# Residual rows and the mixer's first weight tiles loaded behind chosen steps of the down projection

## The chip, the core and the metric

The kernel runs on one core of one Trainium2 chip. The metric is the device time of one execution in microseconds (us); of several executions the median counts. TensorE (PE) does the matrix products, ScalarE (ACT), VectorE (DVE) and GpSimd (POOL) the elementwise work, and SyncE (SP) issues nearly all the transfers between the chip's memory (HBM) and the on-chip SBUF, in one fixed order.

## The reference

One encoder layer in float32 on 1024 rows of 1024 numbers, in three residual blocks and a last norm:

```
x = x + 0.5 * swiglu(rms_norm(x), ffn1_w_in, ffn1_w_out)
x = x + mixer(rms_norm(x), w_in_mix, w_out_mix)
x = x + 0.5 * swiglu(rms_norm(x), ffn2_w_in, ffn2_w_out)
x = rms_norm(x)
```

`swiglu` is `(silu(gate) * up) @ w_out`, with gate and up the halves of `h @ w_in` and an inner width of 2816. The mixer projects the normed rows with `w_in_mix` and runs attention and a gated recurrence on the result. The change touches the two down projections (`@ w_out`) and the loads of the mixer's first weight tiles.

## The kernel before, in words

**Numbers.** Each float32 operand is split into a rounded high part and the rest (`split`, L101): ACT casts the high part (L104), DVE subtracts it from the source for the low part (L105). A product is then three matmuls: high by high, high by low, low by high.

**The down projection** (`ffn_down`, L443) multiplies the 1024 x 2816 activations by the 2816 x 1024 weights. Rows and columns are each halved, and the four quarter results come from seven products in place of eight (the Strassen-Winograd scheme). They run in this order, with their operands' names: A11·B11, A12·B21, S2·T2, A22·T4, S3·T3, S1·T1, S4·B22. Each has 11 steps (`NPAIR`), and a step has 4 row tiles of 3 matmuls, so a product is 132 matmuls. `product` (L524) calls `operands` (L466) for each step, which loads the raw tile of the left operand (`raw_out`, pool `draw`, 4 buffers), loads or builds the right one, and splits both into one of 5 buffers (`ab`; 6 in the second feed-forward block). The left operands A come from `d_act`, the sums S from `d_comb`, both in HBM. Right-hand tiles that serve several products stay in SBUF (`kept` tiles). T2, T4 and T3 are built by POOL from kept tiles (L485 to L495). The profile's names drop the numbers, so A11, A12 and A22 all read `raw_out_ffn_A`, and S1 to S4 read `raw_out_ffn_S`; the PSUM banks tell them apart: `pya` belongs to A11, then S2, then S3, `pyb` to A12, `pyc` to A22, `pyd` to S1, `pye` to S4.

**The residual rows.** The result is added to eight row tiles `x[0]` to `x[7]` of 128 x 1024, on DVE (`add`, L538): the even tiles take A11 and A12, then S2 and S1, the odd ones A22, S3 and S1, and S4 closes the even ones. `rows_in` (L548) loads four of them at a time (512 KB each). It is a hook: a function called after the step whose number it has. The two calls are

```
        product(("A11", "B11"), a, True, {2: [rows_in(0)]})
        product(("A12", "B21"), b, True, {0: [add(0, lo, a)]})
        product(("S2", "T2"), a, False, {0: [add(0, lo, b)], 4: [rows_in(1)]})
```

**The mixer's first weights.** `load_split` (L154) loads a raw tile of 512 KB (L157) into one of three buffers and splits it. `done1` (L1264) asks for two tiles of the recurrence's weights (`raw_rec_w`) once row tile 0 is done; the third and the first tiles of the next projection (`raw_ri_w`) are asked for in the mixer (L639, L688), which PE reaches after the down projection.

**What sets the order.** The program is scheduled when it is built: a planner takes the instructions in the order of the code, with its own idea of time, and writes down a fixed order for each engine. A load with nothing to wait for is moved ahead as far as its buffer and the planner allow, whatever place in the code asked for it. On an engine the order is then fixed: an instruction that waits holds everything behind it, on SP too. `tc.issue_after(ins)` ties what is inside it: it may not be placed ahead of `ins` on that engine. In `operands`, it already keeps the loads of kept tiles behind the step's first load.

## Time and profile before

| what | value |
|---|---|
| median of 3 runs | 2008.72 us (2003.79 to 2009.0) |
| the profiled execution | 2008.14 us |
| its span, first to last instruction | 2006.0 us |
| PE busy | 1944.5 us, 97% of the span |
| DVE, ACT, POOL busy | 1329.7, 807.4, 727.2 us |
| mean granted TensorE clock | 0.991 |
| moved by DMA | 259.34 MB, 129 GB/s on average |

The profiled execution is 2.14 us longer than its span, and 0.58 us shorter than the median. In the timelines, a row is a run of equal instructions: its start, its length, the engine, the line, what is written from what, how often, and in brackets how long the engine had been idle before it and what ended that. SPq stands for SP's queue: a row there is the issue of a transfer, not the transfer. In the rows of windows, a time with (x...) behind it is an engine's busy time and its instruction count; the granted clock, the share of the 16 DMA engines that was busy (just over 1 where the records overlap) and GB/s come last. Line numbers are those of the kernel before.

### The profile page before, as it was taken

What the parts mean: (1) busy time and instruction counts of PE and PEld (TensorE: products, weight loads), DVE (VectorE), ACT (ScalarE), POOL (GpSimd) and SP (SyncE); (2) the same over time, 40 slices, a digit from 0 to 9 for tenths busy, and PEclk for the clock granted to TensorE, in tenths of its full rate; (3) what the DMA queues carried; (4) which work ended last, traced back from release to release, by engine and by line L of the source; (5) the groups of instructions that cost most, each with busy time, mean ns of one, the idle gap of its engine ahead of it and who ended that gap; (6) DMA issues with size and microseconds to landing.
All of it is one profiled execution on the core that took longest, in us unless ns stands there. A gap on an engine that the chain in (4) does not pass through costs nothing.

```text
span 2006.0 us, 26914 instructions
## 1 busy us (share of the span) xinstructions
PE 1944.5 (97%) x10157; PEld 1665.6 (83%) x10157; DVE 1329.7 (66%) x1941; ACT 807.4 (40%) x1269; POOL 727.2 (36%) x543
## 2 busy tenths in 40 slices
...
GB/s 206 142 117 78 116 120 96 79 100 278 303 147 131 152 32 39 47 74 33 105 64 156 138 161 113 64 210 167 138 100 105 105 100 95 77 186 331 184 121 158
DMA packets 219594, 259.34 MB, mean 129 GB/s; under 512 B 12596, under 2 KB 150088, under 8 KB 219464
## 3 DMA queue, kind: packets, MB, share of 16 engines
...
HBM read 185.21 MB, written 72.35 MB: 128 GB/s over the span
## 4 chain that ended last, share of the span: by engine, by line
PE 85%; DMA 6%; DVE 4%; ACT 2%; issue 1%; POOL 1%; SPq 0%; DVEq 0%; ACTq 0%; POOLq 0%
PE pa_ffn L311 16%; PE pd_ffn L311 11%; PE rec_ps L168 6%; PE pya_ffn L515 6%; PE pc_ffn L311 6%; PE pb_ffn L311 5%; PE pye_ffn L515 3%; PE pyd_ffn L515 3%; PE pyc_ffn L515 3%; PE lv L738 2%; PE pa L1032 2%; PE pp_ffn L295 2%; PE ri_ps L649 2%; PE aq_ps L649 2%; PE rg_ps L649 2%; PE py L1032 2%
## 5 line engine op out<-in xcount | busy, mean ns | idle before, releaser
L105 DVE TENSOR_TENSOR hl_in_ffn_A<-raw_in_ffn,hl_in_ffn_A 128x512 fp32r<-128x512 f32 x135 | 200.4, 1489 | 98.6 <-ACT hl_in_ffn_A L104 98.6
L311 PE MATMUL pa_ffn<-ffn_T,hl_in_ffn_S 128*128 128x512 f32 x984 | 242.7, 389 | 0.0
L311 PE MATMUL pd_ffn<-ffn_B,hl_in_ffn_S 128*128 128x512 f32 x960 | 232.7, 389 | 0.0
L311 PEld LDWEIGHTS pa_ffn<-ffn_T,hl_in_ffn_S 128*128 128x128 f32 x984 | 184.7, 188 | 38.4
L311 PEld LDWEIGHTS pd_ffn<-ffn_B,hl_in_ffn_S 128*128 128x128 f32 x960 | 180.2, 188 | 37.4
L105 DVE TENSOR_TENSOR hl_in_ffn_S<-s_ffn,hl_in_ffn_S 128x512 fp32r<-128x512 f32 x164 | 148.0, 907 | 64.1 <-ACT hl_in_ffn_S L104 63.7
L104 ACT CAST hl_in_ffn_S<-s_ffn 128x512 fp32r<-128x512 f32 x164 | 101.6, 622 | 220.2 <-PE pd_ffn L311 167.9
L104 ACT CAST hl_in_ffn_A<-raw_in_ffn 128x512 fp32r<-128x512 f32 x135 | 83.5, 625 | 155.0 <-PE pc_ffn L311 75.0
L105 DVE TENSOR_TENSOR hl_out_ffn_S<-raw_out_ffn_S,hl_out_ffn_S 128x512 fp32r<-128x512 f32 (+1 forms) x88 | 102.8, 1173 | 50.5 <-ACT hl_out_ffn_S L104 50.4
L105 DVE TENSOR_TENSOR hl_out_ffn_A<-raw_out_ffn_A,hl_out_ffn_A 128x1024 fp32r<-128x1024 f32 (+1 forms) x66 | 92.8, 1416 | 55.5 <-ACT hl_out_ffn_A L104 55.0
L273 POOL TENSOR_TENSOR s_ffn<-s_ffn,raw_in_ffn 128x512 f32<-128x512 f32 x41 | 65.7, 1602 | 172.1 <-issue 115.9
L515 PE MATMUL pya_ffn<-hl_out_ffn_S 128*128 128x512 f32 x528 | 122.8, 393 | 4.2 <-DVE hl_out_ffn_S L105 4.2
L168 PE MATMUL rec_ps<-hm,hl_rec_w 128*128 128x512 f32 x528 | 121.6, 390 | 1.9 <-DVE hm L152 1.9
L515 PEld LDWEIGHTS pya_ffn<-hl_out_ffn_S 128*128 128x128 f32 x528 | 100.0, 190 | 26.3 <-DVE hl_out_ffn_S L105 5.5
L311 PE MATMUL pb_ffn<-ffn_B,hl_in_ffn_A 128*128 128x512 f32 x492 | 119.8, 389 | 0.0
L311 PE MATMUL pc_ffn<-ffn_T,hl_in_ffn_A 128*128 128x512 f32 x492 | 118.8, 389 | 0.3 <-DVE hl_in_ffn_A L105 0.3
L311 PE MATMUL pa_ffn<-ffn_B,hl_in_ffn_A 128*128 128x512 f32 x492 | 119.0, 389 | 0.0
L104 ACT CAST hl_out_ffn_S<-raw_out_ffn_S 128x512 fp32r<-128x512 f32 (+1 forms) x88 | 73.5, 837 | 108.4 <-PE pya_ffn L515 41.1
L168 PEld LDWEIGHTS rec_ps<-hm,hl_rec_w 128*128 128x128 f32 x528 | 98.5, 188 | 22.3 <-DVE hm L152 2.2
L311 PEld LDWEIGHTS pc_ffn<-ffn_T,hl_in_ffn_A 128*128 128x128 f32 x492 | 92.3, 188 | 19.8 <-DVE hl_in_ffn_A L105 0.7
L311 PEld LDWEIGHTS pb_ffn<-ffn_B,hl_in_ffn_A 128*128 128x128 f32 x492 | 92.3, 188 | 19.2
L311 PEld LDWEIGHTS pa_ffn<-ffn_B,hl_in_ffn_A 128*128 128x128 f32 x492 | 92.3, 188 | 19.2
...
## 6 DMA issues: line engine op xcount, KB each, us to landing
raw_in_ffn<-in_ffn_w_in SPq DMA_DIRECT2D x88, 512.0 KB, 4.2
raw_out_ffn_S<-d_comb SPq DMA_DIRECT2D x88, 256.0 KB, 2.7
d_comb<-g_ffn POOLq DMA_DIRECT2D x82, 256.0 KB, 2.3
raw_out_ffn_A<-d_act SPq DMA_DIRECT2D x66, 256.0 KB, 5.4
ffn_kept<-in_ffn_w_out SPq DMA_DIRECT2D x65, 256.0 KB, 5.6
d_act<-g_ffn SPq DMA_DIRECT2D x62, 256.0 KB, 2.3
raw_out_ffn_A<-in_ffn_w_out SPq DMA_DIRECT2D x52, 256.0 KB, 4.1
x<-d_x SPq DMA_DIRECT2D x24, 512.0 KB, 5.5
```

The lines of the kernel that those rows point to most:

```text
L104: nc.scalar.copy(hl[:, 0, :], src)
L105: (lo_engine or nc.vector).tensor_sub(hl[:, 1, :], src, hl[:, 0, :].bitcast(F32))
L168: nc.tensor.matmul(out, hl[:, a, ks], h[half][b][:, k, cols], start=(k == 0 and i == 0), stop=(k == NK - 1 and i == 2),)
L273: nc.gpsimd.tensor_sub(s2, s1, a11)
L295: nc.tensor.matmul(halves(ps[j]), A[2 * j + k // 4][:, a, ks], B[k // 4][:, :, b, k % 4, lo:hi], start=(k == 0 and i == 0), stop=(k == NK ...
L311: nc.tensor.matmul(ps, A[:, a, ks], op(key)[:, b, k, :], start=(first and k == 0 and i == 0), stop=(k == 3 and i == 2), skip_group_check=True,
L515: nc.tensor.matmul(ps, hl[:, a, j * P : (j + 1) * P], hl[:, b, hi], start=(first and i == 0 and n == 0), stop=(i == last and n == 2), skip ...
L649: nc.tensor.matmul(ps[:, tt, :], h[half][a][:, k, ts], hl[k // 4][:, b, ws], start=(k == 0 and i == 0), stop=(k == NK - 1 and i == 2),)
L738: nc.tensor.matmul(pl[:, cs], now[:, 0, cs], now[:, 1, cs], start=True, stop=True)
L1032: nc.tensor.matmul(py, lhs(a, n), units[n][:, b, ds], start=(n == 0 and i == 0), stop=(n == 3 and i == 2),)
```

## The change

Three loads get a tie on SP's queue.

- `row_in` loads one row tile behind the raw load of the step at which it is called (`step_load`). `rows_in` now spreads the four calls over the steps 3, 5, 7 and 9 of A11·B11 for the even tiles, and over the same steps of A22·T4 for the odd ones.
- The mixer's first two weight tiles are asked for by a hook, `ahead`, at step 1 of S3·T3, and no longer in `done1`.
- `gate`, set there to that step's raw load, holds every load of `load_split` behind it until the mixer's input part is built. That holds the third recurrence tile and the `raw_ri_w` tiles back too.
- The first add of S3·T3 is called after step 2, not step 0.

The instructions are the same ones in number and size; only orders differ. The diff, without the line that sets `gate` to None at the start:

```
@@ -103,6 +104,10 @@
         nc = self.nc
         nc.scalar.copy(hl[:, 0, :], src)
         (lo_engine or nc.vector).tensor_sub(hl[:, 1, :], src, hl[:, 0, :].bitcast(F32))
+
+    def behind(self, load):
+
+        return self.tc.issue_after(load.ins) if load else nullcontext()
 
     def gain_row(self, name):
         g = self.gpool.tile([P, D], F32, name=f"g_{name}", tag="gain")
@@ -154,7 +159,8 @@
     def load_split(self, src, shape, name, pool=None, tag="whl", lo_engine=None):
 
         raw = self.wpool.tile([P, 1024], F32, name=f"raw_{name}", tag="raw")
-        self.nc.sync.dma_start(raw.rearrange("p (a b) -> p a b", b=shape[1]), src)
+        with self.behind(self.gate):
+            self.nc.sync.dma_start(raw.rearrange("p (a b) -> p a b", b=shape[1]), src)
         hl = (pool or self.wpool).tile([P, 2, 1024], F32R, name=f"hl_{name}", tag=tag)
         self.split(hl, raw, lo_engine)
         return hl
@@ -440,7 +446,7 @@
                 mid()
         next(before)
 
-    def ffn_down(self, name, act, comb, slots, load, done, follow, finish, tail):
+    def ffn_down(self, name, act, comb, slots, load, done, follow, finish, tail, ahead):
 
         nc = self.nc
         w_out = self.io[f"{name}_w_out"]
@@ -467,7 +473,7 @@
             nm = f"{name}_{keys[0]}_{i}"
             left, right = keys
             raw = self.draw.tile([P, 2, 512], F32, name=f"raw_out_{nm}", tag="raw")
-            first = fetch(raw[:, 0], left, i)
+            first = self.step_load = fetch(raw[:, 0], left, i)
             kept = None
             if right == "B11":
                 if i < 4:
@@ -545,19 +551,24 @@
                     )
             return run
 
-        def rows_in(odd):
+        def row_in(t):
             def run():
-                for j in range(4):
-                    x[2 * j + odd] = load(2 * j + odd)
+                with self.behind(self.step_load):
+                    x[t] = load(t)
             return run
 
+        def rows_in(odd, first, hooks):
+            for j in range(4):
+                hooks.setdefault(first + 2 * j, []).append(row_in(2 * j + odd))
+            return hooks
+
         a, b = banks("pya"), banks("pyb")
-        product(("A11", "B11"), a, True, {2: [rows_in(0)]})
+        product(("A11", "B11"), a, True, rows_in(0, 3, {}))
         product(("A12", "B21"), b, True, {0: [add(0, lo, a)]})
-        product(("S2", "T2"), a, False, {0: [add(0, lo, b)], 4: [rows_in(1)]})
+        product(("S2", "T2"), a, False, {0: [add(0, lo, b)]})
         c = banks("pyc")
-        product(("A22", "T4"), c, True, {0: [add(0, hi, a)]})
-        product(("S3", "T3"), a, False, {0: [add(1, lo, c, -1.0)]})
+        product(("A22", "T4"), c, True, rows_in(1, 3, {0: [add(0, hi, a)]}))
+        product(("S3", "T3"), a, False, {1: [ahead], 2: [add(1, lo, c, -1.0)]})
         d = banks("pyd")
         product(("S1", "T1"), d, True, {0: [add(1, lo, a), add(1, hi, a)]})
         e = banks("pye")
@@ -1179,7 +1190,8 @@
         out, x_in = rows(io["out"]), rows(io["x"])
         keys = ("B11", "B21", "T2", "B22", "T4", "T3", "T1")
 
-        def ffn(ctx, name, xn_pair, load, done, d_spec, opened, early_lo, follow, finish, mid=None, tail=2, early=2):
+        def ffn(ctx, name, xn_pair, load, done, d_spec, opened, early_lo, follow, finish, mid=None, tail=2, early=2,
+                ahead=lambda: None):
             def sbuf(c, key, bufs, **kw):
                 return c.enter_context(
                     tc.tile_pool(name=f"{name}_{key}", bufs=bufs, reuse_waits="tile", **kw)
@@ -1213,7 +1225,7 @@
                 slots = [t[:, j, :] for t in tiles for j in range(shape[1])] + extra
                 k.ffn_down(
                     name, act, comb, slots, lambda t: load(pools, t), lambda t, x: done(pools, t, x),
-                    follow, finish, tail,
+                    follow, finish, tail, ahead,
                 )
 
         hstack = ExitStack()
@@ -1265,8 +1277,10 @@
                 nc.sync.dma_start(d["x1"][t], x)
                 xns[t] = pools["xn"].tile([P, D], F32, name=f"xn_n1_{t}", tag="xn")
                 k.norm_rows(x, gain_m[0], xns[t], f"n1_{t}", HALVES)
-                if t == 0:
-                    k.rec_hls = [k.rec_weights(0, j) for j in range(2)]
+
+            def ahead1():
+                k.gate = k.step_load
+                k.rec_hls = [k.rec_weights(0, j) for j in range(2)]
 
             def follow1(t):
                 if not hm:
@@ -1279,12 +1293,13 @@
                     follow1(t)
 
             ffn(c1, "ffn1", pair1, load1, done1, dict(x=8, xn=3), opened1, nc.vector, follow1, finish1,
-                lambda: k.vectors(k.raw), tail=3, early=1)
+                lambda: k.vectors(k.raw), tail=3, early=1, ahead=ahead1)
 
         with ExitStack() as c2:
             pools = open_pools(c2, tc, "m1", st=2, t4=2, v=1, x=1, A=1, rope=1, tot=1, q=2, f=1)
             k.open_psum(c2, "m1", pp=(2, 1024), ph=(2, 1024))
             k.mixer_in(hm, pools, d)
+            k.gate = None
 
         with hstack, ExitStack() as c3:
             pools = open_pools(
```

**Place 1: SP, from the end of the first up projection into A11.** Names carry their numbers here: `raw_out_ffn1_A11_4` is the raw tile of step 4 of A11, `raw_rec_w_0_0` to `_2` are the three recurrence tiles, `ffn1_kept` a kept tile, `d_act21` the last activations going out. Before:

```order
L157 DMA raw_rec_w_0_0_5448<-in_w_in_mix 128x8x128
L157 DMA raw_rec_w_0_1_5453<-in_w_in_mix 128x8x128
L157 DMA raw_rec_w_0_2_5747<-in_w_in_mix 128x8x128
L464 DMA raw_out_ffn1_A11_4_3863<-d_act8_103 128x512
L464 DMA ffn1_kept0_3771<-in_ffn1_w_out 128x512
L464 DMA raw_out_ffn1_A11_5_3883<-d_act10_105 128x512
L464 DMA ffn1_kept0_3771<-in_ffn1_w_out 128x512
L464 DMA raw_out_ffn1_A11_6_3903<-d_act12_107 128x512
L464 DMA ffn1_kept0_3771<-in_ffn1_w_out 128x512
L376 DMA d_act21_116<-g0_ffn1_21_3649 128x512
L464 DMA raw_out_ffn1_A11_7_3923<-d_act14_109 128x512
```

In the changed kernel:

```order
L470 DMA raw_out_ffn1_A11_4_3857<-d_act8_103 128x512
L470 DMA ffn1_kept0_3771<-in_ffn1_w_out 128x512
L470 DMA raw_out_ffn1_A11_5_3877<-d_act10_105 128x512
L470 DMA ffn1_kept0_3771<-in_ffn1_w_out 128x512
L470 DMA raw_out_ffn1_A11_6_3899<-d_act12_107 128x512
L470 DMA ffn1_kept0_3771<-in_ffn1_w_out 128x512
L382 DMA d_act21_116<-g0_ffn1_21_3649 128x512
L470 DMA raw_out_ffn1_A11_7_3919<-d_act14_109 128x512
```

The three recurrence tiles no longer stand ahead of A11's step 4. The three `raw_ri` tiles, which stood behind step 7, are gone from here as well. All six now stand in the S3 product: the recurrence tiles between the raw loads of steps 1 and 2, the `raw_ri` tiles between those of steps 3 and 5. On ACT and on DVE the splits of the recurrence tiles moved from between steps 3 and 4 of A11 to the seam of A22 and S3: tiles 0 and 1 ahead of S3's step 0, tile 2 ahead of its step 1.

**Place 2: SP, in the second half of A12.** `x0_0` to `x0_7` are the residual row tiles. Before:

```order
L464 DMA ffn1_kept2_3773<-in_ffn1_w_out 128x512
L1247 DMA x0_0_3837<-in_x 128x1024
L1247 DMA x0_2_3839<-in_x 128x1024
L1247 DMA x0_4_3841<-in_x 128x1024
L1247 DMA x0_6_3843<-in_x 128x1024
L464 DMA raw_out_ffn1_A12_7_4151<-d_act15_110 128x512
L464 DMA raw_out_ffn1_A12_7_4151<-in_ffn1_w_out 128x512
L464 DMA ffn1_kept2_3773<-in_ffn1_w_out 128x512
L1247 DMA x0_1_4340<-in_x 128x1024
L464 DMA raw_out_ffn1_A12_8_4171<-d_act17_112 128x512
L464 DMA raw_out_ffn1_A12_8_4171<-in_ffn1_w_out 128x512
L464 DMA ffn1_kept2_3773<-in_ffn1_w_out 128x512
```

In the changed kernel:

```order
L470 DMA ffn1_kept2_3773<-in_ffn1_w_out 128x512
L1259 DMA x0_0_3855<-in_x 128x1024
L1259 DMA x0_2_3897<-in_x 128x1024
L1259 DMA x0_4_3939<-in_x 128x1024
L1259 DMA x0_6_3981<-in_x 128x1024
L470 DMA raw_out_ffn1_A12_7_4151<-d_act15_110 128x512
L470 DMA raw_out_ffn1_A12_7_4151<-in_ffn1_w_out 128x512
L470 DMA ffn1_kept2_3773<-in_ffn1_w_out 128x512
L470 DMA raw_out_ffn1_A12_8_4171<-d_act17_112 128x512
L470 DMA raw_out_ffn1_A12_8_4171<-in_ffn1_w_out 128x512
L470 DMA ffn1_kept2_3773<-in_ffn1_w_out 128x512
```

The even tiles stand where they stood, between steps 6 and 7. Of the odd ones, `x0_1` stood here, and the other three stood between these rows and the end of A12; all four stand in A22 now, after the raw loads of steps 3, 5, 7 and 9. In the second block it is the same: the even rows stay at step 6 of A12, the odd ones move from steps 6 and 7 of A12 to A22.

**Place 3: DVE, at the start of S2.** A split of a step of S2 has two subtractions, one from its raw tile and one from its kept tile; `x0_0<-pyb` and the like are the adds of the finished A12 product. Before:

```order
L105 TENSOR_TENSOR hl_out_ffn1_S2_0_4235<-raw_out_ffn1_S2_0_4231,hl_out_ffn1_S2_0_4235 128x512
L542 SCALAR_TENSOR_TENSOR x0_0_3837<-pyb_ffn1_0_3779,x0_0_3837 128x512
L542 SCALAR_TENSOR_TENSOR x0_2_3839<-pyb_ffn1_1_3780,x0_2_3839 128x512
L105 TENSOR_TENSOR hl_out_ffn1_S2_1_4260<-raw_out_ffn1_S2_1_4256,hl_out_ffn1_S2_1_4260 128x512
L542 SCALAR_TENSOR_TENSOR x0_4_3841<-pyb_ffn1_2_3781,x0_4_3841 128x512
L105 TENSOR_TENSOR hl_out_ffn1_S2_0_4235<-ffn1_kept2_3773,hl_out_ffn1_S2_0_4235 128x512
L542 SCALAR_TENSOR_TENSOR x0_6_3843<-pyb_ffn1_3_3782,x0_6_3843 128x512
L105 TENSOR_TENSOR hl_out_ffn1_S2_2_4281<-raw_out_ffn1_S2_2_4277,hl_out_ffn1_S2_2_4281 128x512
L105 TENSOR_TENSOR hl_out_ffn1_S2_1_4260<-ffn1_kept2_3773,hl_out_ffn1_S2_1_4260 128x512
L105 TENSOR_TENSOR hl_out_ffn1_S2_3_4302<-raw_out_ffn1_S2_3_4298,hl_out_ffn1_S2_3_4302 128x512
L105 TENSOR_TENSOR hl_out_ffn1_S2_2_4281<-ffn1_kept3_3774,hl_out_ffn1_S2_2_4281 128x512
```

In the changed kernel:

```order
L106 TENSOR_TENSOR hl_out_ffn1_S2_0_4235<-raw_out_ffn1_S2_0_4231,hl_out_ffn1_S2_0_4235 128x512
L106 TENSOR_TENSOR hl_out_ffn1_S2_1_4260<-raw_out_ffn1_S2_1_4256,hl_out_ffn1_S2_1_4260 128x512
L106 TENSOR_TENSOR hl_out_ffn1_S2_0_4235<-ffn1_kept2_3773,hl_out_ffn1_S2_0_4235 128x512
L106 TENSOR_TENSOR hl_out_ffn1_S2_2_4281<-raw_out_ffn1_S2_2_4277,hl_out_ffn1_S2_2_4281 128x512
L106 TENSOR_TENSOR hl_out_ffn1_S2_1_4260<-ffn1_kept2_3773,hl_out_ffn1_S2_1_4260 128x512
L106 TENSOR_TENSOR hl_out_ffn1_S2_3_4302<-raw_out_ffn1_S2_3_4298,hl_out_ffn1_S2_3_4302 128x512
L548 SCALAR_TENSOR_TENSOR x0_0_3855<-pyb_ffn1_0_3779,x0_0_3855 128x512
L106 TENSOR_TENSOR hl_out_ffn1_S2_2_4281<-ffn1_kept3_3774,hl_out_ffn1_S2_2_4281 128x512
L548 SCALAR_TENSOR_TENSOR x0_2_3897<-pyb_ffn1_1_3780,x0_2_3897 128x512
L548 SCALAR_TENSOR_TENSOR x0_4_3939<-pyb_ffn1_2_3781,x0_4_3939 128x512
L548 SCALAR_TENSOR_TENSOR x0_6_3981<-pyb_ffn1_3_3782,x0_6_3981 128x512
L106 TENSOR_TENSOR hl_out_ffn1_S2_3_4302<-ffn1_kept3_3774,hl_out_ffn1_S2_3_4302 128x512
```

The four adds moved back: both halves of steps 0 and 1 are split ahead of them now, where three of them stood ahead of step 0's second half. In the second block they moved in the same way.

More of the change, by code (lines that the diff above doesn't have):

```diff
@@ L105, in split, with behind @@
         (lo_engine or nc.vector).tensor_sub(hl[:, 1, :], src, hl[:, 0, :].bitcast(F32))
+    def behind(self, load):
+        return self.tc.issue_after(load.ins) if load else nullcontext()
     def gain_row(self, name):
@@ L156, in load_split @@
         raw = self.wpool.tile([P, 1024], F32, name=f"raw_{name}", tag="raw")
-        self.nc.sync.dma_start(raw.rearrange("p (a b) -> p a b", b=shape[1]), src)
+        with self.behind(self.gate):
+            self.nc.sync.dma_start(raw.rearrange("p (a b) -> p a b", b=shape[1]), src)
         hl = (pool or self.wpool).tile([P, 2, 1024], F32R, name=f"hl_{name}", tag=tag)
```

39 lines of the change are left out of this document (23 added, 16 removed).

## Prediction

> **What bounds the kernel now.** I read the page first, then the timeline of PE through both down projections, then the windows and the queues at the places where PE falls behind.
>
> ```profile
> span 2006.0 us, 26914 instructions
> ...
> PE 1944.5 (97%) x10157; PEld 1665.6 (83%) x10157; DVE 1329.7 (66%) x1941; ACT 807.4 (40%) x1269; POOL 727.2 (36%) x543
> ```
>
> PE is the bound. A change of order can win only what PE loses, and the change touches the two down projections alone. PE's timeline there, the first block, then the second:
>
> ```profile
> 463.21 11.04 PE L515 MATMUL pya_ffn<-hl_out_ffn_A 128*128 128x512 f32 x48
> ...
> 494.26 19.20 PE L515 MATMUL pyb_ffn<-hl_out_ffn_A 128*128 128x512 f32 x84
> ...
> 529.10 1.09 PE L515 MATMUL pya_ffn<-hl_out_ffn_S 128*128 128x512 f32 x4
> 532.30 30.89 PE L515 MATMUL pya_ffn<-hl_out_ffn_S 128*128 128x512 f32 x128 [2.11 <-DVE hl_out_ffn_S L105]
> 563.02 30.08 PE L515 MATMUL pyc_ffn<-hl_out_ffn_A 128*128 128x512 f32 x132
> 592.94 30.08 PE L515 MATMUL pya_ffn<-hl_out_ffn_S 128*128 128x512 f32 x132
> ```
>
> ```profile
> 1783.78 30.08 PE L515 MATMUL pya_ffn<-hl_out_ffn_A 128*128 128x512 f32 x132
> 1813.70 22.85 PE L515 MATMUL pyb_ffn<-hl_out_ffn_A 128*128 128x512 f32 x100
> ...
> 1844.66 1.07 PE L515 MATMUL pya_ffn<-hl_out_ffn_S 128*128 128x512 f32 x4
> 1846.84 3.01 PE L515 MATMUL pya_ffn<-hl_out_ffn_S 128*128 128x512 f32 x12 [1.11 <-DVE hl_out_ffn_S L105]
> 1850.82 26.61 PE L515 MATMUL pya_ffn<-hl_out_ffn_S 128*128 128x512 f32 x116 [0.96 <-DVE hl_out_ffn_S L105]
> 1877.26 30.08 PE L515 MATMUL pyc_ffn<-hl_out_ffn_A 128*128 128x512 f32 x132
> ```
>
> Each product is 132 matmuls, so the distance from one product's start to the next is its cost. Undisturbed it is 592.94 - 563.02 = 29.92 us, or 2.72 a step. In the first block A11 takes 31.05, A12 34.84 and S2 33.92: 1.13 + 4.92 + 4.00 = 10.05 us lost. In the second the same three take 29.92, 30.96 and 32.60: 0 + 1.04 + 2.68 = 3.72. The ceiling of the gain is thus 13.77 us. Why PE waits shows in the windows (the last three columns are granted clock, DMA share, GB/s):
>
> ```profile
> 463.00:500.00 37.00, 36.44 (x160) 29.55 (x159) 23.21 (x29) 18.42 (x25) 13.93 (x9) 1.00 1.01 355
> 500.00:531.00 31.00, 27.09 (x112) 20.10 (x110) 21.49 (x17) 10.78 (x13) 16.70 (x11) 1.00 0.98 362
> ...
> 596.00:630.00 34.00, 34.00 (x152) 28.15 (x151) 20.33 (x27) 16.18 (x26) 3.84 (x3) 1.00 0.33 93
> ...
> 1815.00:1850.00 35.00, 33.02 (x143) 26.26 (x142) 23.40 (x20) 12.92 (x17) 18.45 (x13) 1.00 0.94 335
> ```
>
> Through A11 and A12 the DMA engines are full, in S3 two thirds idle. Among what fills them are loads that nobody needs there. SP's queue, and the sizes:
>
> ```profile
> 463.40 2.22 SPq L157 DMA_DIRECT2D raw_rec_w<-in_w_in_mix  x3
> ...
> 473.76 1.70 SPq L157 DMA_DIRECT2D raw_ri_w<-in_w_in_mix  x3
> ...
> 501.59 2.80 SPq L1247 DMA_DIRECT2D x<-in_x  x4
> ...
> 506.29 0.45 SPq L1247 DMA_DIRECT2D x<-in_x  x1
> ...
> 511.40 0.99 SPq L1247 DMA_DIRECT2D x<-in_x  x2
> ...
> 515.38 0.33 SPq L1247 DMA_DIRECT2D x<-in_x  x1
> ```
>
> ```profile
> ffn_kept<-in_ffn_w_out SPq DMA_DIRECT2D x65, 256.0 KB, 5.6
> ...
> x<-in_x SPq DMA_DIRECT2D x16, 512.0 KB, 7.0
> ...
> raw_rec_w<-in_w_in_mix SPq DMA_DIRECT2D x12, 512.0 KB, 3.9
> ```
>
> **The change part by part.** *Mixer tiles out of A11.* ACT shows what they hold up, and SP's own waits what holds them:
>
> ```profile
> 472.44 1.05 ACT L104 CAST hl_rec_w<-raw_rec_w 128x1024 fp32r<-128x1024 f32 x1 [2.15 <-DMA raw_rec_w<-in_w_in_mix]
> 473.40 0.62 ACT L104 CAST hl_out_ffn_A<-raw_out_ffn_A 128x512 fp32r<-128x512 f32 x1
> ...
> 512.82 1.05 ACT L104 CAST hl_out_ffn_A<-raw_out_ffn_A 128x1024 fp32r<-128x1024 f32 x1 [6.10 <-DMA raw_out_ffn_A<-in_ffn_w_out]
> ```
>
> ```profile
> SPq L157 <- DVE hl_ri_w L105: 70.4, 4, 35.6
> ...
> SPq L157 <- PE pa_ffn L311: 15.8, 1, 15.8
> ```
>
> SP stood 15.8 us at the first tile's load, until the up projection's last matmul let its buffer go; step 4 of A11 was queued behind. ACT then cast the three tiles before step 4, which it reached at 473.40, while PE, four steps past 463.21, wanted it at 474.09. Without the tiles, step 4 waits only for its own buffers. I take back all of A11's 1.13 (bounds 0 and 1.13).
>
> *DMA room in A12.* The two windows moved 37 x 355 + 31 x 362 = 24.4 MB. Six mixer tiles and four odd rows of 512 KB are 5.24 MB of it, 14.6 us at 358 GB/s. What stays is 19.1 MB, 53.5 us of DMA in the 62 us that are left when A11 and A12 lose nothing. A12 alone is tighter: 37 loads of 256 KB (the code's three a step, four in the first four) are 9.7 MB, and the four even rows, which do not move, 2.1: 33.0 us of DMA in 29.92 of PE. The 3.1 us over must come from lead, and the buffers allow one: in A22, DVE has split step 8 by 577.01, and PE wants it at 563.02 + 8 x 2.72 = 584.78, 7.8 us later.
>
> ```profile
> 575.23 1.78 DVE L105 TENSOR_TENSOR hl_out_ffn_A<-raw_out_ffn_A,hl_out_ffn_A 128x1024 fp32r<-128x1024 f32 x1 [0.46 <-ACT hl_out_ffn_A L104]
> ...
> 583.39 1.79 DVE L105 TENSOR_TENSOR hl_out_ffn_S<-raw_out_ffn_S,hl_out_ffn_S 128x1024 fp32r<-128x1024 f32 x1 [0.66 <-ACT hl_out_ffn_S L104]
> ```
>
> Of A12's 4.92 I take 4.6 (bounds 0, if the 6.10 us that ACT waited behind the even rows stay, and 4.92). In the second block the eight rows stood together in the window 1815 to 1850; without four of them 2.1 of its 11.7 MB go, 6.3 us at 335 GB/s, against a wait of ACT of 7.41:
>
> ```profile
> 1828.36 1.05 ACT L104 CAST hl_out_ffn_A<-raw_out_ffn_A 128x1024 fp32r<-128x1024 f32 x1 [7.41 <-DMA raw_out_ffn_A<-in_ffn_w_out]
> ```
>
> PE lost only 1.04 by it; I take 1.0 (bounds 0 and 1.04).
>
> *The start of S2.* DVE, and the granted clock right behind PE's gap:
>
> ```profile
> 527.00 1.77 DVE L105 TENSOR_TENSOR hl_out_ffn_S<-raw_out_ffn_S,hl_out_ffn_S 128x512 fp32r<-128x512 f32 x1
> 528.69 1.27 DVE L542 SCALAR_TENSOR_TENSOR x<-pyb_ffn,x 128x512 f32<-128x512 f32 x2
> ...
> 530.49 0.68 DVE L542 SCALAR_TENSOR_TENSOR x<-pyb_ffn,x 128x512 f32<-128x512 f32 x1
> 531.09 1.16 DVE L105 TENSOR_TENSOR hl_out_ffn_S<-ffn_kept,hl_out_ffn_S 128x512 fp32r<-128x512 f32 x1
> ```
>
> ```profile
> 532.00:536.00 4.00, 3.70 (x9) 2.98 (x10) 4.00 (x5) 1.60 (x4) 4.00 (x3) 0.57 0.62 215
> ```
>
> Three adds (1.27 + 0.68) stood ahead of step 0's second half, for which PE waited 2.11. The 128 matmuls behind that gap took 30.72 us; at the pace of 29.92 for 132 they take 29.01, so 1.71 went to the stretch at the lower clock. The second block's gaps of 1.11 and 0.96 lie in or beside a window at 1.00: there no clock was lost.
>
> The Trainium skill (TensorE: Matmul & The Clock Gate, "Why this matters for your kernels") says that gaps of up to about 3 us keep the clock up; the row disagrees, since 2.11 us and the short waits ahead of it were enough. By that rule the low stretch would be unrelated to the gap and stay, and the sum below would be 10.7 (a rival, below).
>
> Now the first add waits for A12's end with the splits from step 2's second half on behind it, where nothing else can pass. With splits of 1.77 and adds of 0.64, step 2 is ready 2.4 us after A12's end (wanted at 5.44), step 3 at 6.1 (8.16), step 4 at 9.6 (10.88), step 5 at 13.2 (13.6), step 6 at 16.7 (16.32); then every step falls 0.82 further back, 3.7 at step 10. With splits of 1.16 a step costs 2.32 and nothing is late. In the slow case each block loses 3.7; I take 0.6 and 0.4, near the quick one, since S2's 128 matmuls above show no further wait with such splits. So S2 gives 4.00 - 0.6 = 3.4 (bounds 0.3 and 4.00) and 2.68 - 0.4 = 2.3 (bounds -1.0 and 2.68).
>
> *Where the loads go.* Six tiles, 3.1 MB, join S3, which moves 93 x 34 = 3.2 MB in its window: 186 GB/s of 358. The odd rows join A22. The tiles' splits stand before S3's steps 0 and 1. SP reaches the tiles when the split of A22's step 8 frees S3's second raw buffer, at 577.0; the third tile landed 472.44 - 463.40 = 9.0 us after the first one's issue with the DMA full, so at 586.0 here; cast 1.05, cast of step 1 1.05, its split 1.79: 589.9, and PE wants it at 595.66. Cost 0, with 5.8 us to spare; past that each us is lost.
>
> The sum: 1.13 + 4.6 + 3.4 + 1.0 + 2.3 = 12.4 us. The profiled execution's 2008.14 (its span and 2.14) becomes 1995.7; from the median of 2008.72, 0.58 higher, it is **1996.3 us**.
>
> **The rivals.** *DVE stays the bound of S2.* For it: DVE is busy 4.00 of 4.00 us in the window at 532. Against: before, 128 matmuls ran behind it without another wait. With 3.7 lost in each block, S2 gives 0.3 and -1.0, the rest 6.7: 6.0 in all, 2002.7.
>
> *A12 stays crowded.* The even rows still stand before step 7, and the lead may not build in 11 steps. Against it: 14.6 us of DMA freed. Then A11 and the moved adds (about 1.9 at the first block's start of S2) give 3.0: 2005.7.
>
> *Slower: the mixer's tiles hold up S3.* ACT and DVE take them in fixed order before steps 0 and 1, and SP has no other way past. It decides at 14.8 us from issue to the third landing. The longest wait of an L157 load, 35.6, in place of 9.0 would cost 35.6 - 14.8 = 20.8, with 1.7 of low clock: 22.5 - 12.4 = 10.1 slower, 2018.8. Against it: S3's window has the DMA two thirds idle, and the three recurrence tiles' buffers are free there. The Trainium skill (DMA: Bandwidth & Descriptors, "Rules for kernel authors") advises issuing a DMA early and waiting late; that is this rival's argument, and A12's full DMA in the trace speaks against it here.
>
> *The low clock stays.* If the stretch near 532 came from something else than PE's gap, its 1.71 us stay lost and the gain is 10.7: 1998.0. Against it: the stretch begins where the gap ends. (This is the clock rule of the Trainium skill quoted above.)
>
> *Nothing happens.* The even rows are meant to spread over A11 and do not move; the rest does. 2008.7.
>
> **How the numbers follow.** My forecast has 0.62, the low clock 0.05, DVE 0.14, crowding 0.11, the slower case 0.05, nothing 0.03. About 0.3%, 6 us, can be told from no change: faster is below 2002.7. The forecast and the low clock, 0.67, count there nearly whole, and of DVE's case about 0.11, where less than the 3.7 is lost: 0.77. Same has crowding and the rests, 0.17; slower 0.06. The ceiling gives 1994.9, and the fastest run before, 2003.79, less 12.4 gives 1991.4; upwards the range takes in DVE's case and stops before crowding: 1991.5 to 2004.
>
> **What would show it.** Right: A11, A12 and S2 each near 29.92 from start to start in both blocks, ACT without the 6.10 and 7.41, no low clock near 532, S3 still 29.92. Wrong: gaps before S2's steps 6 to 10 (DVE), before A12's steps 7 to 10 (crowding), or before S3's steps 0 and 1 (the tiles).

## The result and the profile after

The changed kernel takes 1995.0 us in the median of five runs (1992.53 to 1998.88) against 2008.72 before; the ratio is 0.9940, with a 95% interval of 0.9926 to 0.9954, so 12 us, between 9 and 15. The ratio rests on all the runs, and so differs a little from the quotient of the medians. In a later series on chip 14 it came out the same (after_again below). The first rows of the page:

```profile
span 1997.1 us, 26911 instructions
...
PE 1941.3 (97%) x10157; PEld 1668.0 (84%) x10157; DVE 1338.5 (67%) x1941; ACT 806.7 (40%) x1269; POOL 728.8 (36%) x543
```

The three instructions fewer than before are semaphore instructions. PE's timeline through the two down projections, in three pieces (the lines of the code have moved: the products' L515 is now L521, the splits' L105 is L106, the adds' L542 is L548):

```profile
468.28 30.08 PE L521 MATMUL pya_ffn<-hl_out_ffn_A 128*128 128x512 f32 x132
498.20 30.08 PE L521 MATMUL pyb_ffn<-hl_out_ffn_A 128*128 128x512 f32 x132
528.12 30.08 PE L521 MATMUL pya_ffn<-hl_out_ffn_S 128*128 128x512 f32 x132
558.04 30.08 PE L521 MATMUL pyc_ffn<-hl_out_ffn_A 128*128 128x512 f32 x132
587.96 30.08 PE L521 MATMUL pya_ffn<-hl_out_ffn_S 128*128 128x512 f32 x132
617.88 30.08 PE L521 MATMUL pyd_ffn<-hl_out_ffn_S 128*128 128x512 f32 x132
...
1778.59 30.08 PE L521 MATMUL pya_ffn<-hl_out_ffn_A 128*128 128x512 f32 x132
...
1838.43 30.08 PE L521 MATMUL pya_ffn<-hl_out_ffn_S 128*128 128x512 f32 x132
1868.35 30.08 PE L521 MATMUL pyc_ffn<-hl_out_ffn_A 128*128 128x512 f32 x132
```

Every product from A11 to S1 is one unbroken row, and every start is 29.92 us behind the one before it. All of the 13.77 us that PE lost here is back. Windows of this execution (the one at 563 was not shown of before, and follows):

```profile
463.00:500.00 37.00, 37.00 (x165) 30.64 (x164) 25.39 (x29) 16.45 (x24) 13.65 (x12) 1.00 0.86 299
500.00:531.00 31.00, 31.00 (x138) 25.70 (x137) 25.60 (x18) 12.34 (x16) 20.79 (x13) 1.00 0.89 313
532.00:536.00 4.00, 4.00 (x19) 3.34 (x18) 4.00 (x6) 1.32 (x3) 1.25 (x2) 1.00 0.43 130
563.00:596.00 33.00, 33.00 (x147) 27.33 (x146) 24.39 (x20) 15.39 (x15) 25.73 (x14) 1.00 0.77 244
596.00:630.00 34.00, 34.00 (x152) 28.18 (x151) 23.67 (x30) 16.32 (x28) 5.12 (x3) 1.00 0.42 116
```

Before, the window at 563:

```profile
563.00:596.00 33.00, 33.00 (x147) 27.32 (x146) 22.11 (x20) 12.75 (x13) 22.18 (x15) 1.00 0.44 129
```

The DMA share fell from 1.01 and 0.98 to 0.86 and 0.89 in the first two, and rose in the fourth, from 0.44 to 0.77, where the moved loads now run. This execution is 5 us late, so equal times are not quite equal stages; over A11 and A12 themselves (468.28 to 498.20 to 528.12) the shares are 0.86 and 0.93. The clock behind S2's start is whole.

The span fell by 8.9 us and not by 13.77, because this execution reached A11 at 468.28 and not at 463.21. The order of the instructions up to there is the same in both kernels. The repeat below shows that the late start belongs to this one execution.

### The profile page after: what moved, and what is told of

Read it like the earlier page. It is cut to its first block, busy times and chain, and to the rows that moved or that the text cites. A ratio compares the mean times of both kernels' runs of the same rounds, so it can differ in the third digit from the quotient of the medians.

```text
span 1997.1 us, 26911 instructions
## 1 busy us (share of the span) xinstructions
PE 1941.3 (97%) x10157; PEld 1668.0 (84%) x10157; DVE 1338.5 (67%) x1941; ACT 806.7 (40%) x1269; POOL 728.8 (36%) x543
## 4 chain that ended last, share of the span: by engine, by line
PE 92%; DVE 3%; ACT 2%; DMA 2%; issue 1%; POOL 0%; SPq 0%; DVEq 0%; POOLq 0%; ACTq 0%
PE pa_ffn L317 17%; PE pd_ffn L317 11%; PE pya_ffn L521 9%; PE rec_ps L174 6%; PE pc_ffn L317 6%; PE pb_ffn L317 5%; PE pye_ffn L521 3%; PE pyb_ffn L521 3%; PE pyd_ffn L521 3%; PE pyc_ffn L521 3%; PE pp_ffn L301 3%; PE lv L749 3%; PE pa L1043 2%; PE ri_ps L660 2%; PE aq_ps L660 2%; PE rg_ps L660 2%
## 5 line engine op out<-in xcount | busy, mean ns | idle before, releaser
L106 DVE TENSOR_TENSOR hl_in_ffn_A<-raw_in_ffn,hl_in_ffn_A 128x512 fp32r<-128x512 f32 x135 | 198.8, 1478 | 99.7 <-ACT hl_in_ffn_A L105 99.6
L106 DVE TENSOR_TENSOR hl_in_ffn_S<-s_ffn,hl_in_ffn_S 128x512 fp32r<-128x512 f32 x164 | 148.0, 907 | 64.2 <-ACT hl_in_ffn_S L105 63.6
L105 ACT CAST hl_in_ffn_S<-s_ffn 128x512 fp32r<-128x512 f32 x164 | 101.6, 622 | 220.0 <-PE pd_ffn L317 168.3
L105 ACT CAST hl_in_ffn_A<-raw_in_ffn 128x512 fp32r<-128x512 f32 x135 | 83.4, 624 | 156.3 <-PE pc_ffn L317 75.0
L106 DVE TENSOR_TENSOR hl_out_ffn_S<-raw_out_ffn_S,hl_out_ffn_S 128x512 fp32r<-128x512 f32 (+1 forms) x88 | 107.0, 1226 | 37.9 <-ACT hl_out_ffn_S L105 37.9
L106 DVE TENSOR_TENSOR hl_out_ffn_A<-raw_out_ffn_A,hl_out_ffn_A 128x1024 fp32r<-128x1024 f32 (+1 forms) x66 | 95.0, 1451 | 45.4 <-ACT hl_out_ffn_A L105 44.9
L521 PE MATMUL pya_ffn<-hl_out_ffn_S 128*128 128x512 f32 x528 | 120.3, 390 | 0.0
L521 PEld LDWEIGHTS pya_ffn<-hl_out_ffn_S 128*128 128x128 f32 x528 | 99.2, 188 | 20.5
L105 ACT CAST hl_out_ffn_S<-raw_out_ffn_S 128x512 fp32r<-128x512 f32 (+1 forms) x88 | 73.3, 837 | 98.6 <-PE pya_ffn L521 38.6
```

Source lines behind the costliest of these rows:

```text
L105: nc.scalar.copy(hl[:, 0, :], src)
L106: (lo_engine or nc.vector).tensor_sub(hl[:, 1, :], src, hl[:, 0, :].bitcast(F32))
L521: nc.tensor.matmul(ps, hl[:, a, j * P : (j + 1) * P], hl[:, b, hi], start=(first and i == 0 and n == 0), stop=(i == last and n == 2), skip ...
```

## The experiments

PE's loss in a product is the distance from its start to the next one's, less 29.92. It tells causes apart more finely than the time does. All traces together (us; "rest" is the span less the sum; the ratio is to before on the same chip, over all the runs, with its 95% interval):

| run | A11 at | block 1: A11, A12, S2 | block 2: A11, A12, S2 | sum | span | rest | median | ratio |
|---|---|---|---|---|---|---|---|---|
| before | 463.21 | 1.13, 4.92, 4.00 | 0, 1.04, 2.68 | 13.77 | 2006.0 | 1992.2 | 2008.72 | |
| after | 468.28 | 0, 0, 0 | 0, 0, 0 | 0 | 1997.1 | 1997.1 | 1995.0 | 0.9940 (0.9926 to 0.9954) |
| after_again | 464.45 | 0, 0, 0 | 0, 0, 0 | 0 | 1992.8 | 1992.8 | 1994.79 | 0.9940 (0.9925 to 0.9955) |
| e1_rows | 464.92 | 0.99, 2.06, 1.80 | 0, 0, 0 | 4.85 | 1996.9 | 1992.1 | 2001.36 | 0.9976 (0.9966 to 0.9986) |
| e2_tiles | 464.63 | 0, 0, 2.56 | 0, 0.04, 2.28 | 4.88 | 1998.4 | 1993.5 | 1999.68 | 0.9964 (0.9952 to 0.9976) |
| e3_tiles_a12 | 463.47 | 0, 3.98, 2.18 | 0, 0, 0 | 6.16 | 1997.7 | 1991.5 | 2003.24 | 0.9978 (0.9966 to 0.9990) |
| e4_adds | 464.70 | 0, 0, 5.01 | 0, 0, 1.76 | 6.77 | 1998.4 | 1991.6 | 2002.6 | 0.9986 (0.9974 to 0.9997) |
| e5_tiles_late | 464.21 | 0, 0, 0 | 0, 0, 0 | 0 | 1993.4 | 1993.4 | 1996.44 | 0.9949 (0.9932 to 0.9966) |
| e6_two_adds | 463.18 | 0, 0, 3.52 | 0, 0, 6.70 | 10.22 | 2002.4 | 1992.2 | 2005.32 | 0.9997 (0.9987 to 1.0008) |
| e7_half_first | 464.35 | 0, 0, 2.25 | 0, 0.45, 2.76 | 5.46 | 1999.5 | 1994.0 | 1999.86 | 0.9971 (0.9959 to 0.9983) |
| e4_again | 463.26 | 0, 0, 4.68 | 0, 0, 0.85 | 5.53 | 1998.2 | 1992.7 | 1999.92, one execution | |
| e6_again | 467.13 | 0, 0, 3.28 | 0, 0, 7.21 | 10.49 | 2007.0 | 1996.5 | 2008.82, one execution | |

My theory was that three things had cost time, each by itself: the mixer tiles by their place in A11's order, tiles and rows together by their bytes in A12, and the adds by their place on DVE ahead of S2. The rivals: tiles alone, rows alone, order alone. The later first add of S3 stands in all the experiments and was not tested by itself; S3 lost nothing before the change either.

**e1_rows: the rows moved, the tiles not.** From the changed kernel:

```diff
+                if t == 0:
+                    k.rec_hls = [k.rec_weights(0, j) for j in range(2)]
...
-                lambda: k.vectors(k.raw), tail=3, early=1, ahead=ahead1)
+                lambda: k.vectors(k.raw), tail=3, early=1)
```

> The odd residual rows are queued in A22 as in the changed kernel; the six mixer tiles are asked for in A11, as before the change. Theory A (three separate causes: the tiles hold A11 up by their order, the rows and tiles together crowd the DMA in A12, the order of the adds on DVE makes the gap of S2): the second block, which has no tiles, gets all of its 3.72 us back; in the first A11 still loses about 1.1, A12 1 to 2 (about 22.3 MB, 62 us at 358 GB/s, are left for the two products' 60), S2 0 to 1, so that 2 to 4 us stay lost of 13.77 and the time is about 1998. Rival (the tiles alone crowd the first block): A12's 4.9 and S2's 4.0 stay there, only the second block gains: about 2005.

PE in the first block:

```profile
464.92 11.04 PE L521 MATMUL pya_ffn<-hl_out_ffn_A 128*128 128x512 f32 x48
476.14 1.20 PE L521 MATMUL pya_ffn<-hl_out_ffn_A 128*128 128x512 f32 x4 [0.18 <-ACT hl_out_ffn_A L105]
...
515.75 1.20 PE L521 MATMUL pyb_ffn<-hl_out_ffn_A 128*128 128x512 f32 x4 [0.72 <-ACT hl_out_ffn_A L105]
517.72 10.25 PE L521 MATMUL pyb_ffn<-hl_out_ffn_A 128*128 128x512 f32 x44 [0.76 <-DVE hl_out_ffn_A L106]
```

The second block lost nothing, and the first 0.99, 2.06 and 1.80. This fits theory A better than the rival, which left the first block its 4.9 and 4.0; but A12 and S2 lost more than the 1 to 2 and 0 to 1 expected, 4.85 in all for 2 to 4, and the time came out 3 us above 1998. The gap at 476.14, at A11's step 4, I put down to the tiles' place in the order, those at step 7 of A12 to their bytes; e3_tiles_a12 tests this.

**e2_tiles: the tiles moved, the rows not.** The rows' hooks as before the change:

```diff
-        product(("A11", "B11"), a, True, rows_in(0, 3, {}))
+        product(("A11", "B11"), a, True, {2: [rows_in(0)]})
...
-        product(("S2", "T2"), a, False, {0: [add(0, lo, b)]})
+        product(("S2", "T2"), a, False, {0: [add(0, lo, b)], 4: [rows_in(1)]})
```

> The six mixer tiles are queued in S3 as in the changed kernel; the residual rows are loaded as before the change. Theory A: A11 gets its 1.1 us back, A12 loses 0 to 1.5 (21.3 MB, 59.5 us at 358 GB/s), S2 of the first block still loses 2 to 4 (the three adds stand ahead of its step 0's second half on DVE, as before), the second block keeps all of its 3.72: about 2002.5. Rival (the rows alone crowd A12): only A11's 1.1 comes back, about 2007.6.

A11 and A12 lost nothing, though SP still issued all eight residual rows in A12: without the tiles there was lead enough. S2 lost 2.56 and 2.28. The rival, by which only A11's 1.1 comes back, fell. I had expected the second block to lose the 3.72 that it lost before; it lost 2.32, with 0.04 for 1.04 in A12. With the same loads A12 of that block lost 0.45 in e7_half_first, so this small term probably varies from one execution to the next.

**e3_tiles_a12: the tiles gated to A12.**

```diff
-        product(("A12", "B21"), b, True, {0: [add(0, lo, a)]})
+        product(("A12", "B21"), b, True, {0: [add(0, lo, a)], 1: [ahead]})
...
-        product(("S3", "T3"), a, False, {1: [ahead], 2: [add(1, lo, c, -1.0)]})
+        product(("S3", "T3"), a, False, {2: [add(1, lo, c, -1.0)]})
```

> The rows are queued as in the changed kernel; the six mixer tiles are gated to A12's steps 1 to 7 instead of S3. Theory A (bytes on a full DMA): A12 needs 33.0 us of DMA and 8.8 more for six tiles, 42 in its 29.92 with about 8 us of lead from a quiet A11: A12 and S2 together lose 3 to 8 us, no other product any. Rival (what costs is only that the tiles stand ahead of a step of A11 on ACT and SP while SP waits for a buffer, not their bytes): at most 0.5 us lost.

```profile
493.39 19.20 PE L521 MATMUL pyb_ffn<-hl_out_ffn_A 128*128 128x512 f32 x84
514.39 1.20 PE L521 MATMUL pyb_ffn<-hl_out_ffn_A 128*128 128x512 f32 x4 [1.80 <-ACT hl_out_ffn_A L105]
516.37 3.03 PE L521 MATMUL pyb_ffn<-hl_out_ffn_A 128*128 128x512 f32 x12 [0.78 <-DVE hl_out_ffn_A L106]
519.91 7.55 PE L521 MATMUL pyb_ffn<-hl_out_ffn_A 128*128 128x512 f32 x32 [0.51 <-DVE hl_out_ffn_A L106]
```

A12 and S2 lost 6.16 us (3 to 8 expected), and A11 none. From A12's start to S2's the DMA share was 1.02 (359 GB/s), for 0.93 in the changed kernel, and ACT waited 3.99 and 6.10 us for the raw tiles of A12's steps 6 and 7, for 1.67 and 6.16 there. So the tiles cost time there too, and not only by their place ahead of a step of A11: the rival falls. Their bytes fit what was seen; their splits, which moved with them, were not tested apart.

**e4_adds: the loads as in the changed kernel, the old order of the adds.** S2's step 0 second half is put behind the third add (second block: the first):

```diff
-                self.split(hl[:, :, hi], kept)
+                with self.behind(self.held if right == "T2" and i == 0 else None):
+                    self.split(hl[:, :, hi], kept)
...
-        product(("S2", "T2"), a, False, {0: [add(0, lo, b)]})
+        add(0, lo, b)()
+        self.held = self.adds[2 if name == "ffn1" else 0]
+        product(("S2", "T2"), a, False, {})
```

> All loads as in the changed kernel; on DVE alone the second half of S2's step 0 is put behind three adds in the first block and behind one in the second, as it stood before the change. Theory A (the order of the adds makes S2's gap, and the gap the low clock): the gap of the first block is 3 x 0.64 + 1.77 less the 0.9 us that PE works on the first half, about 2.8 us, and 1.7 of half clock behind it, 4.5 lost; in the second 0.64 + 1.77 - 0.9 = 1.5 without low clock; 6 in all over the changed kernel. Rival (the gap of S2 came from loads that were late): nothing lost. On the clock: if the low stretch comes although no other wait stands near, the gap alone is enough for it; if it stays away, the short waits ahead of the gap were needed.

```profile
524.54 1.07 PE L522 MATMUL pya_ffn<-hl_out_ffn_S 128*128 128x512 f32 x4
528.69 30.94 PE L522 MATMUL pya_ffn<-hl_out_ffn_S 128*128 128x512 f32 x128 [3.08 <-DVE hl_out_ffn_S L106]
```

Only S2 lost, 5.01 and 1.76, for 4.5 and 1.5 expected. The order of a few instructions on DVE is enough to make the gap, with the loads of the changed kernel.

**e7_half_first: the loads of e2_tiles, the adds behind the second half.**

```diff
-        product(("S2", "T2"), a, False, {0: [add(0, lo, b)], 4: [rows_in(1)]})
+        def adds():
+            with self.behind(self.half):
+                add(0, lo, b)()
+        product(("S2", "T2"), a, False, {0: [adds], 4: [rows_in(1)]})
```

> The mixer tiles as in the changed kernel, the residual rows loaded as before the change (in e2_tiles S2 lost 2.6 and 2.3 us with these loads), but on DVE the second half of S2's step 0 is put ahead of the four adds in both blocks. Theory A, revised by e2_tiles (with the tiles gone the rows crowd nothing; they act through the order of the adds alone): 0 to 0.7 us lost in each S2, nothing in A12, so about 1995. Rival (the rows' bytes still make S2's loads late): S2 loses 1 to 2.5 in each block though the adds are out of its way.

Theory A, as I had revised it, fell: S2 still lost 2.25 and 2.76. PE at S2's start, and DVE from the last split of A12 on:

```profile
524.19 1.07 PE L523 MATMUL pya_ffn<-hl_out_ffn_S 128*128 128x512 f32 x4
526.32 3.01 PE L523 MATMUL pya_ffn<-hl_out_ffn_S 128*128 128x512 f32 x12 [1.07 <-DVE hl_out_ffn_S L106]
529.92 26.61 PE L523 MATMUL pya_ffn<-hl_out_ffn_S 128*128 128x512 f32 x116 [0.58 <-DVE hl_out_ffn_S L106]
```

DVE:

```profile
519.25 1.93 DVE L106 TENSOR_TENSOR hl_out_ffn_A<-raw_out_ffn_A,hl_out_ffn_A 128x1024 fp32r<-128x1024 f32 x1 [1.32 <-ACT hl_out_ffn_A L105]
521.10 3.48 DVE L106 TENSOR_TENSOR hl_out_ffn_S<-raw_out_ffn_S,hl_out_ffn_S 128x512 fp32r<-128x512 f32 x2
524.51 1.76 DVE L106 TENSOR_TENSOR hl_out_ffn_S<-ffn_kept,hl_out_ffn_S 128x512 fp32r<-128x512 f32 x1
526.19 2.47 DVE L550 SCALAR_TENSOR_TENSOR x<-pyb_ffn,x 128x512 f32<-128x512 f32 x4
528.59 0.67 DVE L106 TENSOR_TENSOR hl_out_ffn_S<-raw_out_ffn_S,hl_out_ffn_S 128x512 fp32r<-128x512 f32 x1
529.19 0.68 DVE L106 TENSOR_TENSOR hl_out_ffn_S<-ffn_kept,hl_out_ffn_S 128x512 fp32r<-128x512 f32 x1
```

And in the changed kernel (after_again):

```profile
507.51 8.64 DVE L106 TENSOR_TENSOR hl_out_ffn_A<-raw_out_ffn_A,hl_out_ffn_A 128x1024 fp32r<-128x1024 f32 x4 [1.73 <-ACT hl_out_ffn_A L105]
516.07 3.47 DVE L106 TENSOR_TENSOR hl_out_ffn_S<-raw_out_ffn_S,hl_out_ffn_S 128x512 fp32r<-128x512 f32 x2
519.46 1.78 DVE L106 TENSOR_TENSOR hl_out_ffn_S<-ffn_kept,hl_out_ffn_S 128x512 fp32r<-128x512 f32 x1
```

PE starts S2 at 524.19 and 524.29. DVE is done with A12 at 521.18 in the one, 3.0 us ahead, and at 516.15 in the other, 8.1 ahead; before the change it was 2.0 (527.07 for 529.10). Up to the second half of S2's step 0 DVE has three splits to do, 3.48 + 1.76 = 5.2 us. With 8.1 us of lead they fit. With 3.0 and the 1.07 that PE works on the first half they come 1.1 us late, as measured (1.07), whatever stands behind them. With the odd rows back in A12 its DMA share was 0.97 (363 GB/s), for 0.92 (331 GB/s) in after_again. The rows thus take away DVE's lead into S2. The gap at step 0 has two causes, and each is enough by itself.

This holds for the first gap only. The second, 0.58, is at step 1, whose second half (the row at 529.19) stood behind the four adds. From start to start, the first gap cost 1.2 us in each block (2.13 and 2.16 for 4 matmuls that take 0.91), and the second 0.9 and 1.4. How much of the second is lead and how much the adds was not tested.

The same sum for before, as an estimate with splits of this length: 5.2 - 2.0 of lead - 1.09 of PE's work is 2.1 us. That would make its whole gap of 2.11 even without the adds.

**after_again: the changed kernel once more.**

> The changed kernel once more, for the part of the time that lies outside the down projections. In the first runs the span less what PE lost in them was 1992.2 before the change and 1991.5 to 1993.5 in four experiments, but 1997.1 in the profiled execution of the changed kernel, which reached A11 at 468.28 (463.2 to 464.9 in the others). Theory A (a late start-up in that one execution): A11 starts at 463 to 465, every product is 29.92 apart, the span is 1991.5 to 1993.5. Rival (the change makes the start-up slower): A11 again near 468, span near 1997.

```profile
464.45 30.08 PE L521 MATMUL pya_ffn<-hl_out_ffn_A 128*128 128x512 f32 x132
```

Theory A: A11 at 464.45, nothing lost, a span of 1992.8. Where the first execution fell behind shows in the same window of both, after and then after_again:

```profile
65.00:80.00 15.00, 11.40 (x38) 8.45 (x37) 13.40 (x12) 6.45 (x12) 12.51 (x9) 0.77 0.30 88
```

```profile
65.00:80.00 15.00, 13.01 (x56) 10.14 (x56) 12.83 (x11) 7.60 (x14) 12.36 (x9) 1.00 0.40 116
```

In this window PE did 38 matmuls for 56, at a clock of 0.77, after it had waited for an up projection tile. The only other late A11 (e6_again, 467.13) shows 0.77 in this window too.

**e5_tiles_late: the tiles at the last product's step 7.**

```diff
-        product(("S3", "T3"), a, False, {1: [ahead], 2: [add(1, lo, c, -1.0)]})
+        product(("S3", "T3"), a, False, {2: [add(1, lo, c, -1.0)]})
...
-        hooks = {0: [add(1, hi, d), add(0, hi, d)]}
+        hooks = {0: [add(1, hi, d), add(0, hi, d)], 7: [ahead]}
```

> All as in the changed kernel, but the six mixer tiles are asked for at S4's step 7, the last product, instead of S3. Theory A (the tiles must be behind the full DMA but still before DVE's busiest stretch): all products keep their 29.92; at the seam from S4 to the mixer the three splits of the recurrence tiles stand amid the norms on DVE, and PE waits up to 3 x 1.23 = 3.7 us more there. Rival (later is as good, since the norms leave DVE time): nothing more lost.

```profile
681.68 3.68 PE L153 MATMUL pt_n<-ident,xn_n 128*128 128x128 f32 x16 [4.28 <-DVE xn_n L137]
...
701.24 0.49 PE L174 MATMUL rec_ps<-hm,hl_rec_w 128*128 128x512 f32 x1 [0.29 <-ACT hm L156]
```

No product lost anything. At the seam PE waited 4.28 for a norm, and reached the first `rec_ps` 57.5 us behind S4's start (643.73), for 54.2 in after_again: 3.3 later, near the 3.7 expected. The low clock may have part in this: it was at 0.50 from 680.0 to 690.2, and whole there in after_again. By the start of the second down projection 0.9 of it was left (1774.84 - 643.73 = 1131.1 from the start of S4, for 1774.23 - 643.98 = 1130.3); where the rest came back isn't shown. The median is 1.65 higher, but the intervals overlap. S3 is the better place, by a little at most.

**e6_two_adds, e4_again, e6_again: the gap and the clock.** In e6_two_adds and e6_again one pair of numbers of e4_adds is changed (e4_again is e4_adds unchanged):

```diff
-        self.held = self.adds[2 if name == "ffn1" else 0]
+        self.held = self.adds[1 if name == "ffn1" else 2]
```

> All loads as in the changed kernel; on DVE the second half of S2's step 0 is put behind two adds in the first block (in the run of e4_adds behind three) and behind three, with two splits between them, in the second. The order's price: a gap of 2 x 0.64 + 1.77 - 0.9 = 2.15 in the first block, 3 x 0.64 + 2 x 1.77 + 1.77 - 0.9 = 6.3 at most in the second (4.1 if the splits between are quick ones). On the clock, theory A (the gap alone sets the low stretch, from about 2 us on; 3.08 did in e4_adds, 1.60 and 1.80 with short waits beside them did not in two others): a low stretch of 1.7 to 1.9 us loss behind both gaps. Rival (about 3 us are needed, and before the change the waits of A12 helped): none behind the 2.15.

> The kernel of e4_adds once more, for the clock alone. Theory A, formed on the ten traces so far: the granted clock is set anew every 3.413 us, on a grid that runs through the whole execution, and it is halved for a step when PE stood idle for more than about 0.56 of the step before (below 0.49 it never was). A gap of about 3.1 us (0.91 of a step) at S2 then costs a low stretch or none by where it falls on the grid: low when one step holds over 1.9 us of it, none when the grid cuts it near its middle. Rival (the length of the gap decides, or the waits near it): the same gap gives the same clock as in e4_adds, a low stretch behind the first block's gap, wherever the grid stands.

> The kernel of e6_two_adds once more, for the clock alone. Theory A (as for e4_again): in the first block the gap of about 3.2 us was cut by the grid into 0.47 and 0.48 of a step and cost no low stretch; here it does when one step holds over 0.56 of idle time, and again none when both lie below 0.49. The second block's gap of 4.8 us always fills over half of some step and always costs a low stretch. Rival (length or neighbourhood decides): none behind the first gap and one behind the second, as in e6_two_adds, wherever the grid stands.

The first block's gap in e6_two_adds was 3.23, and not 2.15: a split of 1.24 us stood between the adds, which my price had left out; the second block's was 4.80, for 4.1 to 6.3. No low stretch came behind the first, though both the 2 us of theory A and the 3 us of the rival were passed; both fell. With the gaps in order of length, the low stretch came behind 2.11 (before) and 2.79 (e4_again), not behind 2.94 (e6_again), behind 3.08 (e4_adds), not behind 3.23 (e6_two_adds), and behind 4.80 and 5.38 (the second blocks of e6_two_adds and e6_again). Length does not sort them. The grid, the theory that I formed after that and stated ahead of the two repeats, does. Windows of one step, laid on the grid by another low stretch of the same trace: first e4_adds, then e6_two_adds (the columns are as ahead; the second is PE's busy time, the third from the end the clock):

```profile
526.26:529.67 3.41, 0.98 (x4) 0.85 (x5) 3.41 (x6) 0.00 (x0) 2.73 (x3) 1.00 0.42 153
529.67:533.08 3.41, 3.41 (x9) 2.68 (x9) 2.70 (x5) 1.14 (x2) 0.26 (x1) 0.50 0.18 56
```

```profile
522.31:525.72 3.41, 1.78 (x8) 1.13 (x6) 3.41 (x4) 1.14 (x2) 2.91 (x3) 1.00 0.62 207
525.72:529.14 3.42, 1.83 (x8) 1.53 (x9) 3.42 (x6) 0.00 (x0) 2.29 (x2) 1.00 0.24 85
529.14:532.55 3.41, 3.41 (x17) 2.83 (x16) 2.32 (x4) 1.47 (x3) 0.00 (x0) 1.00 0.52 169
```

In the first, one step holds the gap and PE is idle for 71% of it: the next runs at 0.50. In the second the grid cuts the longer gap, and PE is idle for 48% and 46% of two steps, and the clock stays. In before the step was idle for 61%:

```profile
528.85:532.27 3.42, 1.34 (x6) 0.74 (x4) 3.42 (x6) 2.22 (x5) 3.42 (x3) 1.00 0.85 252
532.27:535.68 3.41, 3.38 (x8) 2.71 (x9) 3.41 (x4) 1.32 (x3) 3.41 (x3) 0.50 0.59 199
```

The two repeats by themselves do not tell the theories apart, for each kernel came out as it had the first time: 82% in one step and low in e4_again, 54% and 32% and not low in e6_again. It is all the gaps together that speak against length.

## Why the prediction was right

*The sum.* Forecast 12.4 us and 1996.3; measured 1995.0. PE got back 13.77 in the trace. The medians differ by 13.7 in the first runs and by 10.9 in the later ones (2005.72 to 1994.79), the ratio gives 12. The trace of before, at 2008.14, lies above its medians in the later runs (2006.91 and 2005.72), so its 13.77 may be more than a median execution loses; this wasn't shown.

*Mixer tiles out of A11: 1.13.* Measured 1.13, and 0.99 came back as a loss when the tiles alone stayed. Right.

*DMA room in A12: 4.6 and 1.0.* Measured 4.92 and 1.04. The mechanism was right, and its sign was not: I named the end of ACT's waits of 6.10 and 7.41 as the proof. They are still there:

```profile
511.05 1.05 ACT L105 CAST hl_out_ffn_A<-raw_out_ffn_A 128x1024 fp32r<-128x1024 f32 x1 [6.16 <-DMA raw_out_ffn_A<-in_ffn_w_out]
...
1821.37 1.05 ACT L105 CAST hl_out_ffn_A<-raw_out_ffn_A 128x1024 fp32r<-128x1024 f32 x1 [6.08 <-DMA raw_out_ffn_A<-in_ffn_w_out]
```

ACT still waits for this cast as long as before. But this cast, for step 7, now starts 42.8 us behind A11's start (511.05 - 468.28), and 49.6 before; PE wants the step at 498.20 + 7 x 2.72 = 517.2. The wait was not removed, it was covered by lead. How the 4.92 splits: moving the tiles alone gives it all back (e2_tiles), moving the rows alone 2.9 (e1_rows left 2.06). They overlap, and a sum of single effects would have counted too much.

*The start of S2: 3.4 and 2.3.* Measured 4.00 and 2.68. The step that failed is the cause: "Three adds (1.27 + 0.68) stood ahead of step 0's second half, for which PE waited 2.11." The order of the adds was one of two causes; the other, DVE's short lead into S2, does not appear in the sum. e4_adds shows that the order suffices, e7_half_first that without it a gap of 1.07 stays at step 0, and by the estimate there the lead alone gives all 2.11 of before. The change removed both causes, so the number held; as to the cause that was luck, for by that estimate a change of the order alone would have left the gap. Nor did S2 fall back later, for which I had kept 0.6 and 0.4: with DVE 7.4 us ahead (520.76 for 528.12) S2 runs through without a wait. *DVE as the bound of S2* is out by that.

*Where the loads go: 0.* Right; S3 runs unbroken from 587.96. The splits of the tiles and of S3's steps 0 and 1 on DVE:

```profile
578.52 2.23 DVE L106 TENSOR_TENSOR hl_rec_w<-raw_rec_w,hl_rec_w 128x1024 fp32r<-128x1024 f32 x1
581.24 1.75 DVE L106 TENSOR_TENSOR hl_rec_w<-raw_rec_w,hl_rec_w 128x1024 fp32r<-128x1024 f32 x1 [0.48 <-ACT hl_rec_w L105]
582.91 1.21 DVE L106 TENSOR_TENSOR hl_out_ffn_S<-raw_out_ffn_S,hl_out_ffn_S 128x1024 fp32r<-128x1024 f32 x1
584.05 1.22 DVE L106 TENSOR_TENSOR hl_rec_w<-raw_rec_w,hl_rec_w 128x1024 fp32r<-128x1024 f32 x1
585.18 3.45 DVE L106 TENSOR_TENSOR hl_out_ffn_S<-raw_out_ffn_S,hl_out_ffn_S 128x1024 fp32r<-128x1024 f32 x2
```

Step 1 is ready at 585.18 + 1.73 = 586.9 and wanted at 587.96 + 2.72 = 590.7. The spare time is 3.8, not 5.8. The slower rival needed a delay past the spare time, and did not come. The Trainium skill (DMA: Bandwidth & Descriptors, "Rules for kernel authors") advises issuing early. Here e1_rows and e3_tiles_a12 lost 4.85 and 6.16 with loads that were early and in a full stretch, and e5_tiles_late, with the latest place, about 3 at the seam, of which 0.9 was left later: in this kernel early paid where the DMA had room.

*The low clock.* It went with the gap, as forecast. The Trainium skill (TensorE: Matmul & The Clock Gate, "Why this matters for your kernels") asks for no gaps above about 3 us. As a border this does not fit: gaps of 2.11 and 2.79 cost a low stretch here, one of 3.23 did not. The same page ("What's actually happening") says that the clock gate watches a window of 3413 ns that runs free of the program, and with that the traces agree: the low stretches of a trace all begin on one grid of 3.413 us, and end on it too, save the one that the end of the trace cuts off.
